# Hybrid encoder layer: one more pair of input columns ahead of the scan, gates clipped inside the scan step, level 8 issued behind level 64, low parts of filler weights apart

## The chip, the cores and the metric

The kernel runs on one core of a Trainium2 chip. The metric is the device time of one execution in microseconds. Before the change it was 1707.46 us, the median of three runs (1707.11 to 1707.71).

## What is computed

One layer on x of 1024 tokens by 1024 channels, in float32:

```
h    = RMSNorm(x);  P = h @ W_in      # 1024 -> 8192 columns
A    = pointwise(silu(LayerNorm(dwconv31(GLU(P_glu)))))
B    = bidirectional gated scan over 8 heads of 128
       S_t = diag(f_t) S_{t-1} + k_t v_t^T,  o_t = S_t^T q_t
       f = clip(lb + (1 - lb) sigmoid(z), 1e-6, 1),  k = (1 - lb) sigmoid(-z)
       then RMSNorm per head * silu(out gate), @ o_w
x    = x + W_out(sigmoid(gA) * A + sigmoid(gB) * B)
x    = x + W_down(silu(dwconv3(h2 W_gate)) * (h2 W_up)),  h2 = RMSNorm(x)
out  = RMSNorm(x)
```

## The kernel before

**Products.** For TensorE (PE) each operand is split into a high part and a low part of type float32r: `split` (L125) casts the high part on ScalarE (ACT) and subtracts it on VectorE (DVE) for the low part. `mm3` issues three matmuls of 512 columns for one product of 128 x 128 weights with 512 tokens: high by high (L149), high by low (L150), low by high (L151). The program counts its PE work in **pieces** of six such matmuls. A column tile of 128 outputs over all 1024 tokens is 8 pieces (48 matmuls) with `std_job` (L251). `pair_job` (L293) does two column tiles together by a Strassen-Winograd scheme of seven products in place of eight: 14 pieces (84 matmuls) in place of 16 (96), with more sums of tiles around them, on DVE, on ACT and, for pairs that are not "first", by accumulating DMAs that GpSimd (POOL) issues (L302).

**Order.** PE's order is the order in which the program issues (`manual_schedule`); the other engines' orders are made by a scheduler, except where `pin` or `issue_after` hold an instruction. A `Stream` is a generator of pieces; `fill(n)` issues n of them, and n may be a fraction that accumulates. So constants such as `FILL` say how much dense work is put between two steps of something else.

**Stages.** The first norm and its transposes (from 0 us; in `warm` and ahead of it PE runs matmuls on a constant that nobody reads, while it waits for x); the GLU tiles (to about 110 us); the depthwise convolution of 31 taps, which DVE does as 120 multiply-adds of 1024 columns (L1065) while PE works through the pairs of the input projection (`conv_steps`, `CONV_FILL` pieces for each tap); the LayerNorm of the convolution with the last pairs (`conv_norm`, to about 475 us); then the scan (from about 498 to 850 us), and after it the output projection, the merge, W_out, the FFN and the last norm.

The 56 column tiles of the input projection that GLU doesn't take are the list `todo`. The first 2 x `NPAIRS` = 38 go through pairs ahead of the scan, and the other 18 (`rest`) are filler within the scan, as `std_job`s, together with the 8 column tiles of the pointwise product.

**The scan.** There are 16 steps, one for each head and each half (512) of the tokens. For both directions at once a chunk is doubled from level to level: at level h, keys kG and queries qF of blocks of h tokens are multiplied by block totals tb (`double_keys`, `double_queries`, `totals`, all recorded at L1194 through `tt`), and ACT copies interleaved pages of them (`woven`, L1228) for PE's small matmuls of the scores (`level`, L1247). Level 1 to 16 are `scan_base`, a generator of five steps; levels 32 and 64 are `scan_levels`, and `scan_states` transposes the level-64 keys (L1382, copied by ACT at L1385), multiplies them with the values (L1392), and makes forward and backward states (L1400, L1410 and then L1491). When both halves of a head are done, `scan_outputs` multiplies the scores and states (L1433, half 1 first), takes squares on ACT (L1438), a power on POOL (L575, L576), scales the result on ACT (L1452), transposes it (L1460) and gates it on DVE (L1462).

Three steps are interleaved by hand. In the step of half i, `between(n)` is called five times; each call issues `FILL` pieces of filler, one step of the outputs of the head before (`pending`), and one step of the base of a following half: the first step (n = 4) of half i + 2, and steps two to five (n = 0 to 3) of half i + 1. `scan_inputs` loads q and the gates' z, and ACT makes kG (L1215), the sigmoid (L1216) and f (L1217); DVE clips f there (L1218). In `Base.step` the first step is held behind the level-64 keys of the half at hand:

```python
            while n > 0 and self.val is None:
                if self.first and last_keys:
                    with tc.issue_after(last_keys[0].ins):
                        self.val = next(self.gen)
```

Halves alternate. While the scores of a half 0 are under way PE does the output matmuls L1433 of the head before, for its half 0, and afterwards their transposes L1460; below, an **A-half** is the stretch from the end of those L1433 to the scores `sc` L1247 of the next half.

Of the kernel before, what the change touches and what calls it, by code (L numbers as in the profile page):

```python
# [10 lines left out]
F32 = mybir.dt.float32  # L11
# [5 lines left out]
AX = mybir.AxisListType  # L17

P = 128
FILL = 1.77  # L20
TAIL = ((1, 2), (1, 1), (2, 4), (2, 3))
CONV_FILL = 1.53
NPAIRS = 19
LN_MEAN = 5
GLU_FIRST = 4
GLU_LEAD = 6
GLU_FILL = 2
GLU_MORE = 4
GLU_LATE = 17
WARM = ((2, 0), (1, 3), (2, 6), (4, 8))  # L30
ALIGN = 128
AHEAD = 55
H = 512
EPS = 1e-6
MIN_FORGET = 1e-6
# [13 lines left out]
def tile_hybrid_encoder(  # L49
# [74 lines left out]
    def split(hi, lo, src, eng, late=False):  # L124
        parts = A.copy(hi, src), eng.tensor_tensor(lo, src, hi.bitcast(F32), op=ALU.subtract)  # L125
        if late:
            for i in parts:
                pin(i)
        return hi, lo
# [9 lines left out]
    def w_page(nk, pool=None):  # L139
        if pool is None:  # L140
            return mp.tile([P, nk, P], F32R, tag="wp", name=nm("wp"), bufs=4)
        return pool.tile([P, nk, P], F32R, tag="wq", name=nm("wq"), bufs=3)
# [105 lines left out]
            while not self.done:  # L248
                self.fill()

    def std_job(src, nk, acts, evac, halves=(0, 1), step=2):  # L251


        def prep():
            raw = raw_w(src, nk)
            return split(w_page(nk), w_page(nk), raw, V)

        def run(w, halves=halves):
            for half in halves:
                acc = bank("mm")  # L260
                for k in range(nk):
                    mm3(acc, w, acts(k, half), k, k == 0, k == nk - 1)
                    if k % step == step - 1 or k == nk - 1:
                        yield
                evac(half, acc)

        return prep, run
# [297 lines left out]
    def in_cols(c0):  # L565
        return w_cols(w_in, 0, ND, c0)
# [570 lines left out]


    rest = todo[2 * NPAIRS :]
    rest_jobs = [std_job(in_cols(c), ND, h_std, e) for c, e in rest[:-2]]  # L1140
    (c0, e0), (c1, e1) = rest[-2:]
    rest_jobs.append(duo_job(in_cols(c0), in_cols(c1), ND, h_std, e0, e1))
    ca = [[None, None] for _ in range(NCW)]
# [30 lines left out]
        return loads, run  # L1174

    rest_jobs.append(pw_first())
    rest_jobs += [std_job(pw_col(i), NCW, ca_of, gated_a(i)) for i in range(1, ND - 2)]
    rest_jobs.append(
        duo_job(pw_col(ND - 2), pw_col(ND - 1), NCW, ca_of, gated_a(ND - 2), gated_a(ND - 1))
    )  # L1180
# [23 lines left out]
    def scan_inputs(i):  # L1204


        h, half = divmod(i, 2)
        q = page(hp, "q", 2)
        f = hp.tile([P, 2, H], F32, tag="f", name=nm("f"), bufs=2)
        kG = hp.tile([P, 2, H], F32, tag="kG", name=nm("kG"), bufs=3)  # L1210
        nc.sync.dma_start(q, d_q[h][half])
        for d in range(2):
            z = page(hp, "zi", 3)
            nc.sync.dma_start(z, d_z[d][h][half])
            A.activation(kG[:, d, :], z, AF.Sigmoid, scale=-1.0)  # L1215
            A.activation(z, z, AF.Sigmoid)  # L1216
            A.activation(f[:, d, :], z, AF.Identity, scale=oml_of(d, h), bias=lb_of(d, h))  # L1217
        V.tensor_scalar(f, f, MIN_FORGET, 1.0, op0=ALU.max, op1=ALU.min)  # L1218
        return q, f, kG, kscale[:, h : h + NH + 1 : NH]

    def pairs(t, h, other=H):
# [47 lines left out]
    def scan_base(ins):  # L1269
# [7 lines left out]
        k_d, Q1 = page(hp, "A", 8), page(hp, "A", 8)  # L1277
        tt(k_d, kG[:, 0, :], kG[:, 1, :], ALU.add)
        A1 = woven(kG, 1)
        odd = H // 2  # L1280
        tt(
            pairs(Q1, 1, 0),
# [185 lines left out]

    class Base:
        def __init__(self, ins):  # L1470
            self.gen, self.val, self.first = scan_base(ins), None, True

        def step(self, n):
            while n > 0 and self.val is None:
                if self.first and last_keys:
                    with tc.issue_after(last_keys[0].ins):
                        self.val = next(self.gen)
                else:
                    self.val = next(self.gen)
                self.first = False  # L1480
                n -= 1

        def result(self):
# [643 lines left out]
```

## Time and profile before

| what | value |
|---|---|
| median of the runs | 1707.46 us (1707.11 to 1707.71) |
| the profiled execution's own time | 1706.98 us |
| its span, first to last instruction | 1705.0 us |
| granted TensorE clock, mean | 0.999 |
| PE busy | 1688.6 us, 11719 rows of matmuls |
| DVE busy | 1269.3 us |
| ACT busy | 827.3 us |
| POOL busy | 245.9 us |
| DMA, mean over the span | 180 GB/s |

Times in rows of a timeline are the start and the duration of an instruction in microseconds. The duration of a matmul includes its way through the array, so what one costs in a row of them is read from start to start. "[0.59 <-ACT A L1228]" behind a row is the idle time of its engine ahead of it and the instruction that ended it. A line number is that of the kernel before.

### The profile page before, as it was taken

What the parts mean: (1) busy time and instruction counts of PE and PEld (TensorE: products, weight loads), DVE (VectorE), ACT (ScalarE), POOL (GpSimd) and SP (SyncE); (2) the same over time, 40 slices, a digit from 0 to 9 for tenths busy, and PEclk for the clock granted to TensorE, in tenths of its full rate; (3) what the DMA queues carried; (4) which work ended last, traced back from release to release, by engine and by line L of the source; (5) the groups of instructions that cost most, each with busy time, mean ns of one, the idle gap of its engine ahead of it and who ended that gap; (6) DMA issues with size and microseconds to landing.
All of it is one profiled execution on the core that took longest, in us unless ns stands there. A gap on an engine that the chain in (4) does not pass through costs nothing.

```text
span 1705.0 us, 30406 instructions
## 1 busy us (share of the span) xinstructions
PE 1688.6 (99%) x11719; PEld 1408.2 (83%) x11719; DVE 1269.3 (74%) x1938; ACT 827.3 (49%) x1562; POOL 245.9 (14%) x287
## 2 busy tenths in 40 slices
PE   9999999999999999999999999999999999999998
PEld 6788888888888888888888888888888888888787
DVE  5889899887678888888565467676777776657865
ACT  7454343335476777776432345444344434442334
POOL 1312222200001111111100003122222222000110
PEclk9999999999999999999999999999999999999999
DMA  7887887866573444436797455686777776773842
GB/s 240 284 213 186 191 196 172 205 187 206 165 236 100 139 129 134 129 116 221 241 294 243 128 167 176 153 171 143 172 164 178 164 183 149 237 260 102 212 98 99
DMA packets 332871, 306.17 MB, mean 180 GB/s; under 512 B 17454, under 2 KB 244918, under 8 KB 332726
## 3 DMA queue, kind: packets, MB, share of 16 engines
q1 hardware_dynamic: 285366, 265.42, 48.8%
q0 software_dynamic: 47360, 38.81, 15.4%
q8 instruction: 92, 1.51, 0.4%
q14 instruction: 53, 0.43, 0.1%
HBM read 201.40 MB, written 84.93 MB: 168 GB/s over the span
## 4 chain that ended last, share of the span: by engine, by line
PE 70%; ACT 1%; DVE 1%; DMA 0%; issue 0%; POOL 0%; POOLq 0%; ACTq 0%; DVEq 0%
PE mm L149 16%; PE mm L151 16%; PE mm L150 16%; PE sc L149 3%; PE sc L150 3%; PE sc L151 3%; PE ob L1433 2%; PE tr L149 2%; PE tr L150 2%; PE tr L151 2%; PE sc L1247 1%; PE sc L1333 1%; PE mm L1392 1%; PE sc L1392 1%; PE ob L1247 1%; PE tr L1382 0%
## 5 line engine op out<-in xcount | busy, mean ns | idle before, releaser
L149 PE MATMUL mm<-hx,wp 128*128 128x512 f32 x1068 | 425.7, 399 | 0.0
L151 PE MATMUL mm<-hx,wp 128*128 128x512 f32 x1068 | 417.0, 390 | 0.5 <-DVE wp L125 0.5
L150 PE MATMUL mm<-hx,wp 128*128 128x512 f32 x1068 | 416.2, 390 | 0.6 <-POOL hx L125 0.6
L125 ACT CAST wp<-wr 128x1024 fp32r<-128x1024 f32 (+2 forms) x146 | 146.9, 1006 | 224.3 <-PE mm L150 165.0
L151 PEld LDWEIGHTS mm<-hx,wp 128*128 128x128 f32 x1068 | 200.5, 188 | 44.6 <-DVE wp L125 1.6
L149 PEld LDWEIGHTS mm<-hx,wp 128*128 128x128 f32 x1068 | 200.6, 188 | 40.6 <-ACT wp L125 0.2
L150 PEld LDWEIGHTS mm<-hx,wp 128*128 128x128 f32 x1068 | 200.8, 188 | 39.9 <-POOL hx L125 1.0
L125 DVE TENSOR_TENSOR wp<-wr,wp 128x1024 fp32r<-128x1024 f32 (+2 forms) x144 | 169.5, 1177 | 39.8 <-ACT wp L125 39.4
L1065 DVE SCALAR_TENSOR_TENSOR acc<-gl,v_b,acc 128x1024 f32<-128x1024 f32 x120 | 153.5, 1280 | 1.7
L441 ACT COPY su<-mm 128x512 f32<-128x512 f32 x82 | 47.8, 583 | 84.4 <-PE mm L151 84.3
L1371 POOL DMA_DIRECT2D S<-D x64 | 36.1, 571 | 281.1 <-ACT jk L1438 125.3
L125 ACT CAST wq<-sw 128x1024 fp32r<-128x1024 f32 x41 | 43.2, 1054 | 61.3 <-PE mm L150 32.9
L1194 DVE TENSOR_TENSOR qF<-qF,tb 128x512 f32<-128x512 f32 x96 | 65.9, 686 | 9.5 <-ACT A L1228 8.9
L149 PE MATMUL tr<-hx,wp 128*128 128x512 f32 x180 | 70.1, 390 | 0.0
L151 PE MATMUL tr<-hx,wp 128*128 128x512 f32 x180 | 70.1, 389 | 0.0
L150 PE MATMUL tr<-hx,wp 128*128 128x512 f32 x180 | 70.0, 389 | 0.0
L1194 DVE TENSOR_TENSOR kG<-kG,tb 128x512 f32<-128x512 f32 x96 | 65.9, 687 | 4.0 <-ACT A L1228 2.2
L1710 DVE SCALAR_TENSOR_TENSOR tm<-gp,v_a,tm 128x512 f32<-128x512 f32 x88 | 66.0, 750 | 3.3 <-ACT tm L1708 1.3
L302 POOL DMA_DIRECT2D sw<-in_ffn_w_up_dram x38 | 49.8, 1502 | 116.0 <-DMA sw<-in_ffn_w_up_dram 72.4
L149 PE MATMUL sc<-hy,wq 128*128 128x512 f32 x164 | 63.9, 390 | 0.0
L151 PE MATMUL mm<-hy,wp 128*128 128x512 f32 x164 | 63.8, 389 | 0.0
L149 PE MATMUL mm<-hy,wp 128*128 128x512 f32 x164 | 63.8, 389 | 0.0
(377 smaller groups left out, 3721.9 us busy)
## 6 DMA issues: line engine op xcount, KB each, us to landing
wr<-in_w_in_dram SPq DMA_DIRECT2D x48, 512.0 KB, 5.6
wr<-in_ffn_w_up_dram SPq DMA_DIRECT2D x22, 512.0 KB, 5.6
sw<-in_w_in_dram SPq DMA_DIRECT2D x38, 256.0 KB, 3.1
d_g<-ft SPq DMA_DIRECT2D x38, 256.0 KB, 2.0
sw<-in_ffn_w_up_dram SPq DMA_DIRECT2D x38, 256.0 KB, 3.2
sw<-in_ffn_w_up_dram POOLq DMA_DIRECT2D x38, 256.0 KB, 6.7
wr<-sw POOLq DMA_DIRECT2D x32, 256.0 KB, 3.2
wr<-wr POOLq DMA_DIRECT2D x32, 256.0 KB, 3.3
```

Of the source, the lines that this page charges most:

```text
L125: parts = A.copy(hi, src), eng.tensor_tensor(lo, src, hi.bitcast(F32), op=ALU.subtract)
L149: T.matmul(acc, whi[:, k, :], ahi, start=first, stop=False, skip_group_check=again)
L150: T.matmul(acc, whi[:, k, :], alo, start=False, stop=False, skip_group_check=again)
L151: T.matmul(acc, wlo[:, k, :], ahi, start=False, stop=last, skip_group_check=again)
L302: G.dma_start(o, a, accum_op=ALU.add)
L441: A.copy(t, acc)
L1065: V.scalar_tensor_tensor(acc, g[:, k : k + S], tap(k), acc, op0=ALU.mult, op1=ALU.add)
L1194: return V.tensor_tensor(o, a, b, op=op)
L1247: T.matmul(b[g, o], A_t[:, at : at + 32], Q_t(at), start=True, stop=True)
L1371: G.dma_start(S_t[g : g + 32, :, g : g + 32], D_t[g : g + 32])
L1392: T.matmul(u[:, sl], kTs[d][:, sl], v[:, c, :], start=True, stop=True)
L1710: V.scalar_tensor_tensor(c, g[:, o + k : o + k + H], vec("fdw", k * NF + j), c, op0=ALU.mult, op1=ALU.add,)
```

## The change

- `NPAIRS` 19 to 20: two column tiles leave the filler and become a twentieth pair, ahead of the scan; `CONV_FILL` 1.53 to 1.64 spreads the pairs over the taps.
- `FILL` 1.77 to 1.57: less filler between the steps of the scan.
- `std_job` gets `apart`: for the filler jobs but the first (and the duo), the cast to the high part is issued two pieces after the load, and the subtraction for the low part a piece later, where both were issued with the load.
- The clip of f moves from `scan_inputs` into `scan_base`, behind the copy of the level-1 keys.
- `Base.step` holds the fourth step (masks of the near levels, the doubling of level 8, the pages of level 16) behind the level-64 keys of the half at hand as well.
- At the start 104 instead of 55 small matmuls run ahead of x, and none instead of two wide ones behind them.

```diff
-FILL = 1.77
+FILL = 1.57
-CONV_FILL = 1.53
-NPAIRS = 19
+CONV_FILL = 1.64
+NPAIRS = 20
-WARM = ((2, 0), (1, 3), (2, 6), (4, 8))
+WARM = ((0, 0), (1, 3), (2, 6), (4, 8))
-AHEAD = 55
+AHEAD = 104
...
-    def std_job(src, nk, acts, evac, halves=(0, 1), step=2):
+    def std_job(src, nk, acts, evac, halves=(0, 1), step=2, apart=False):
         def prep():
             raw = raw_w(src, nk)
-            return split(w_page(nk), w_page(nk), raw, V)
+            if not apart:
+                return split(w_page(nk), w_page(nk), raw, V)
+            hi, lo = w_page(nk), w_page(nk)
+            def low():
+                V.tensor_tensor(lo, raw, hi.bitcast(F32), op=ALU.subtract)
+            def high():
+                A.copy(hi, raw)
+                later(1, low)
+            later(2, high)
+            return hi, lo
...
-    rest_jobs = [std_job(in_cols(c), ND, h_std, e) for c, e in rest[:-2]]
+    rest_jobs = [std_job(in_cols(c), ND, h_std, e, apart=n > 0) for n, (c, e) in enumerate(rest[:-2])]
...
-    rest_jobs += [std_job(pw_col(i), NCW, ca_of, gated_a(i)) for i in range(1, ND - 2)]
+    rest_jobs += [std_job(pw_col(i), NCW, ca_of, gated_a(i), apart=True) for i in range(1, ND - 2)]
...
-        V.tensor_scalar(f, f, MIN_FORGET, 1.0, op0=ALU.max, op1=ALU.min)
         return q, f, kG, kscale[:, h : h + NH + 1 : NH]
...
         A1 = woven(kG, 1)
+        V.tensor_scalar(f, f, MIN_FORGET, 1.0, op0=ALU.max, op1=ALU.min)
...
-            self.gen, self.val, self.first = scan_base(ins), None, True
+            self.gen, self.val, self.at = scan_base(ins), None, 0
...
-                if self.first and last_keys:
+                if self.at in (0, 3) and last_keys:
                     with tc.issue_after(last_keys[0].ins):
                         self.val = next(self.gen)
                 else:
                     self.val = next(self.gen)
-                self.first = False
+                self.at += 1
```

In the changed kernel the lines from `std_job` on stand 12 further down, those between the clip's old and new place 11, and those behind it 12 again. DVE's order in an A-half late in the scan, before: f is the forget gate of the half after next, kG_7922 and qF_8241 the keys and queries of the half at hand (shapes x8x32 level 32, x4x64 level 64), kG_8263 and qF_8620 those of the next half (x128x2 level 2, x64x4 level 4, x32x8 level 8), wp the low part of a filler weight, ev the gated output, D the scores.

```order
L1218 TENSOR_SCALAR f_8636<-f_8636 128x1024
L1194 TENSOR_TENSOR kG_7922<-kG_7922,tb_8584 128x2x8x32
L1194 TENSOR_TENSOR qF_8241<-qF_8241,tb_8584 128x2x8x32
L1194 TENSOR_TENSOR kG_8263<-kG_8263,tb_8633 128x2x128x2
L1194 TENSOR_TENSOR qF_8620<-qF_8620,tb_8633 128x2x128x2
L1194 TENSOR_TENSOR kG_8263<-kG_8263,tb_8735 128x2x64x4
L1194 TENSOR_TENSOR qF_8620<-qF_8620,tb_8735 128x2x64x4
L1462 SCALAR_TENSOR_TENSOR ev_8775<-tr_8770,v_a,og_8541 128x512
L125 TENSOR_TENSOR wp_8754<-wr_8751,wp_8753 128x1024
L1194 TENSOR_TENSOR kG_8263<-kG_8263,tb_8845 128x2x32x8
L1311 COPY_PREDICATED D_8621<-m_d,sc_8778 128x128
L1194 TENSOR_TENSOR kG_7922<-kG_7922,tb_8711 128x2x4x64
```

The same place on DVE now; the half at hand is kG_8033 and qF_8341, the next one kG_8364 and qF_8720:

```order
L1206 TENSOR_TENSOR kG_8033<-kG_8033,tb_8688 128x2x8x32
L1206 TENSOR_TENSOR qF_8341<-qF_8341,tb_8688 128x2x8x32
L1206 TENSOR_TENSOR kG_8364<-kG_8364,tb_8734 128x2x128x2
L1206 TENSOR_TENSOR qF_8720<-qF_8720,tb_8734 128x2x128x2
L1206 TENSOR_TENSOR kG_8364<-kG_8364,tb_8829 128x2x64x4
L1206 TENSOR_TENSOR qF_8720<-qF_8720,tb_8829 128x2x64x4
L1474 SCALAR_TENSOR_TENSOR ev_8863<-tr_8858,v_a,og_8635 128x512
L1206 TENSOR_TENSOR kG_8033<-kG_8033,tb_8811 128x2x4x64
L1206 TENSOR_TENSOR qF_8341<-qF_8341,tb_8811 128x2x4x64
L1323 COPY_PREDICATED D_8721<-m_d,sc_8866 128x128
L1206 TENSOR_TENSOR kG_8364<-kG_8364,tb_8933 128x2x32x8
```

The clip is gone from the head of the row, and the level-64 keys stand ahead of the level-8 keys, a masked copy and the low part of a filler weight, which all stood ahead of them.

PE's order at the end of the first A-half, before: mm is filler, and the transposes of the outputs (tr, from tm) stand right ahead of the scores.

```order
L150 MATMUL mm_5876<-hx_691,wp_5529 128x512
L151 MATMUL mm_5876<-hx_690,wp_5530 128x512
L149 MATMUL mm_5876<-hx_710,wp_5529 128x512
L150 MATMUL mm_5876<-hx_711,wp_5529 128x512
L151 MATMUL mm_5876<-hx_710,wp_5530 128x512
L149 MATMUL mm_5876<-hx_730,wp_5529 128x512
L150 MATMUL mm_5876<-hx_731,wp_5529 128x512
L151 MATMUL mm_5876<-hx_730,wp_5530 128x512
L149 MATMUL mm_5876<-hx_750,wp_5529 128x512
L150 MATMUL mm_5876<-hx_751,wp_5529 128x512
L151 MATMUL mm_5876<-hx_750,wp_5530 128x512
L1460 MATMUL tr_5918<-ident,tm_5685 128x128 x4
```

The same place on PE now, with the transposes of the values (tr from tm_5955) at the head:

```order
L1556 MATMUL tr_6049<-ident,tm_5955 128x128 x4
L149 MATMUL mm_6020<-hx_988,wp_5479 128x512
L150 MATMUL mm_6020<-hx_989,wp_5479 128x512
L151 MATMUL mm_6020<-hx_988,wp_5480 128x512
L149 MATMUL mm_6020<-hx_1060,wp_5479 128x512
L150 MATMUL mm_6020<-hx_1061,wp_5479 128x512
L151 MATMUL mm_6020<-hx_1060,wp_5480 128x512
L1472 MATMUL tr_6062<-ident,tm_5843 128x128 x4
```

Between the transposes of the values and those of the outputs stands one piece of filler here, where two stood. Over the whole A-half, from the end of L1433 to the scores, the order has seven pieces in each of the six A-halves before, and now six, six, seven, six, six, seven. PE's 512-column matmuls number 84 more ahead of the scan and 96 fewer within it.

ACT's order in an A-half, from the copy of the outputs to the level-4 pages (tm L1435 and its squares L1438, kT L1385, a page L1228, an input L1215, L1216, L1217 here and there, the scales L1452, then the pages of levels 2 and 4), has the same instructions before and now, but for the cast of a filler weight that stood in some of them.

## Prediction

> **What bounds the kernel now.** First the page: the shares of the engines.
>
> ```profile
> span 1705.0 us, 30406 instructions
> PE 1688.6 (99%) x11719; PEld 1408.2 (83%) x11719; DVE 1269.3 (74%) x1938; ACT 827.3 (49%) x1562; POOL 245.9 (14%) x287
> ```
>
> PE is busy for 1688.6 of 1705.0 us, so the time is PE's work plus the few waits that it has. Work is priced from start to start: two rows of the timeline with six 512-column matmuls from the one to the other.
>
> ```profile
> 429.62 0.39 PE L150 MATMUL mm<-hy,wq 128*128 128x512 f32 x1
> 430.98 0.39 PE L150 MATMUL mm<-hy,wq 128*128 128x512 f32 x1
> ```
>
> (430.98 - 429.62) / 6 = 0.2267 us for a matmul, so 1.36 us for a piece of six. The Trainium skill, in "TensorE: Matmul & The Clock Gate", section "Wait — 56ns, not 53.3ns?", gives 215.7 ns for 512 columns on the full clock; this trace has 226.7, and the measurement decides.
>
> Next the waits of PE, longest sums first; the columns are total, times, longest.
>
> ```profile
> PE mm L502 <- DMA vr<-in_attn_norm_w_dram: 2.3, 1, 2.3
> PE tr L1382 <- DVE kG L1194: 1.4, 2, 1.1
> ...
> PE sc L1247 <- ACT A L1228: 0.6, 1, 0.6
> ```
>
> Two lines are of the scan: the level-64 keys from DVE (1.4) and the interleaved pages from ACT (0.6), 2.0 us together. The first is the start and isn't touched. So the scan is tight, but PE hardly ever waits in it. The chain of waits says by what it is tight: in an A-half it leaves PE.
>
> ```profile
> 558.84 2.47 PE ob L1433 x22
> 561.33 0.60 ACT tm L1435
> ...
> 565.42 1.67 POOL ors L576
> ...
> 567.88 0.88 ACT tm L1452 x3
> ...
> 575.25 0.53 ACT A L1228
> 575.80 0.59 DVE qF L1194
> ...
> 580.40 0.55 PE tr L1382 x3
> ```
>
> From the end of the output matmuls at 561.33 the work goes through ACT, POOL's power, ACT's scales, the gates' inputs and pages, to the level-4 page at 575.78: 14.45 us, in which PE has only its filler to do. From there DVE carries it to the level-64 keys and PE waits at 580.40.
>
> **The change part by part.**
>
> *Work.* The pair adds 84 matmuls ahead of the scan and the scan loses 96: 12 x 0.2267 = 2.72 us less. Nothing hides that, PE being the bound: -2.72.
>
> *The pair ahead of the scan.* It needs sums and casts on DVE, beside the taps.
>
> ```profile
> 83.00:370.00 287.00, 287.00 (x1268) 237.73 (x1267) 251.23 (x250) 111.62 (x153) 56.89 (x52) 1.00 0.80 192
> ```
>
> The taps' group on the page:
>
> ```profile
> L1065 DVE SCALAR_TENSOR_TENSOR acc<-gl,v_b,acc 128x1024 f32<-128x1024 f32 x120 | 153.5, 1280 | 1.7
> ```
>
> In the stretch of the taps PE is busy without a gap (287.00 of 287.00) and DVE for 251.23, 88%. A pair takes 84 x 0.2267 = 19.0 us, and 287 / 19.0 = 15.1 pairs share the stretch. Taps aside DVE does (251.23 - 153.5) / 15.1 = 6.5 us for one. With a pair more it has some 258 us in 306, 84%: less dense than before. I price it at 0, hidden by PE's own 19 us; bounds: a gain is excluded, since PE has no gap there to lose, and if its cover is gone once, a tap (1.28) is what stands ahead of a part, so +1.3.
>
> *The start.* More small matmuls, no wide ones.
>
> ```profile
> 2.49 1.65 PE L681 MATMUL mm<-ident 128*32 128x32 bf16 x55
> 4.07 1.03 PE L678 MATMUL mm<-ident 128*128 128x512 bf16 x2
> 4.90 0.43 PE L667 MATMUL sc<-ident,xt 128*128 128x128 f32 x1
> 6.76 0.42 PE L667 MATMUL tr<-ident,xt 128*128 128x128 f32 x1
> 6.97 0.37 PE L667 MATMUL ob<-ident,xt 128*128 128x128 f32 x1
> ...
> 8.50 0.27 PE L667 MATMUL sc<-ident,xt 128*128 128x128 f32 x1
> 8.61 0.27 PE L667 MATMUL tr<-ident,xt 128*128 128x128 f32 x1
> ...
> 10.61 0.49 PE L664 MATMUL mm<-diag,ones_r 128*128 128x128 f32 x2 [0.74 <-DVE rs L652]
> ```
>
> A small one costs (4.07 - 2.49) / 55 = 0.0287, so 104 end at 2.49 + 2.99 = 5.48 and the first transpose of x starts 0.58 later than 4.90. That is hidden by the 0.74 at 10.61, a wait for sums of squares that come from ACT and DVE and not from these transposes: 0. Without that cover it is +0.58.
>
> *Old waits of the scan.* Two things made them. At 580.40 PE waited for the level-64 keys; now these stand ahead of the level-8 keys and of the filler's low part, and the clip no longer stands ahead of everything. At 747.36 the clip had held up DVE:
>
> ```profile
> 743.15 0.70 DVE L1218 TENSOR_SCALAR f<-f 128x1024 f32<-128x1024 f32 x1 [2.21 <-ACT f L1217]
> 747.36 0.46 PE L1247 MATMUL sc<-A,A 128*32 128x32 f32 x32 [0.59 <-ACT A L1228]
> ```
>
> DVE stood 2.21 us behind ACT's f, for a clip that only a later half needs; the keys of levels 2 and 4 queued behind it, ACT's pages behind those, PE behind the pages. The clip's new place is behind the keys' scaling, where f has long been written. I take the whole 2.0 off: -2.0; bounds -2.0 and 0. Behind the level-64 keys the fourth step now waits, with masks and level 8; its pages are asked for only in the next half, so it is priced at 0 here and counts in DVE's share below.
>
> *Casts apart.* Cast and subtraction are the same instructions later. A weight tile is loaded a job ahead, 8 or 16 pieces, and the low part is issued after three: five pieces, 5 x 1.36 = 6.8 us at least, are left as cover. 0.
>
> *What is late next.* PE takes the A-half in less time, and the chain through ACT is as long as it was. Four A-halves, each with PE's scores and ACT's last page that these need (a page of qF, in the last third of the 96 small matmuls):
>
> ```profile
> 575.32 0.46 PE L1247 MATMUL sc<-q,A 128*32 128x32 f32 x32
> 575.59 1.07 PE L1247 MATMUL sc<-A,A 128*32 128x32 f32 x96
> ...
> 618.35 1.04 PE L1247 MATMUL sc<-A,A 128*32 128x32 f32 x94
> ...
> 661.18 1.07 PE L1247 MATMUL sc<-A,A 128*32 128x32 f32 x96
> ...
> 703.76 0.46 PE L1247 MATMUL sc<-q,A 128*32 128x32 f32 x32
> 704.03 0.96 PE L1247 MATMUL sc<-A,A 128*32 128x32 f32 x84
> ```
>
> ```profile
> 575.14 0.63 ACT L1228 COPY A<-qF 128x512 f32<-128x512 f32 x1
> 618.20 0.62 ACT L1228 COPY A<-qF 128x512 f32<-128x512 f32 x1
> 660.40 0.62 ACT L1228 COPY A<-qF 128x512 f32<-128x512 f32 x1
> 702.84 0.62 ACT L1228 COPY A<-qF 128x512 f32<-128x512 f32 x1
> ```
>
> The last third starts some 0.59 behind the first row (64 of 96 in 1.07 less a tail of 0.2). So the page was early by 575.59 + 0.59 - 575.77 = 0.41, then 618.94 - 618.82 = 0.12, 661.77 - 661.02 = 0.75, 704.62 - 703.46 = 1.16 us. One piece less, 1.36, in the first, second, fourth and fifth of six A-halves leaves PE waiting 0.95, 1.24 and 0.20 in the first, second and fourth. The third and sixth keep seven pieces: 0. The fifth (747.36) was 0.59 late and loses 1.36, 1.95 together, but the 2.21 behind f go: 0. Sum +2.4. Bounds: 0, if the cast that stood in some of these chains goes and the scheduler's order gains as much; 2.4 + 1.95 = 4.4, if the clip's idle time only changes its place.
>
> *DVE's share.* Here is the sum row of the stretches from 520 to 850 us.
>
> ```profile
> sum 330.00, PE 328.02 PEld 282.06 DVE 277.81 ACT 236.15 POOL 47.43; mean PE 109.34 PEld 94.02 DVE 92.61 ACT 78.72 POOL 15.81
> ```
>
> A period of two halves (one head) is (703.76 - 575.32) / 3 = 42.8 us, and DVE works 277.81 / 330 x 42.8 = 36.0 of it. Two pieces fewer in each of eight periods leave 42.8 - 2.7 = 40.1 for the same 36.0: 90%. No row shows PE's waits at that density. Below 0 is excluded, since no PE wait is left for it to save; the upper end is the second rival. The nearest row is the stretch of the taps, with 88% and no gap on PE, which speaks for little: I take 0.15 a head, +1.2.
>
> Sum against the profiled execution: 1706.98 - 2.72 - 2.0 + 2.4 + 1.2 = 1705.86. The median of the runs was 1707.46, 0.48 above that execution, so the forecast is 1706.3 us, 0.07% less than before.
>
> **The rivals.**
>
> *All waits vanish.* ACT's chain is shorter by 1.24 us or more in each A-half and DVE's density costs nothing: 1707.46 - 2.72 - 2.0 = 1702.7, faster. For it: POOL's power alone is 1.67 of the chain, so half of that gap filled with casts or inputs would do. Against: ACT's instructions in the chain are the same. It counts as faster by over 0.2% (3.4 us, about what a measurement of this kernel can tell from no change) with new waits under 1.3 us.
>
> *DVE becomes the scan's clock, and the time is longer.* DVE idled 42.8 - 36.0 = 6.8 us a period, in waits of which these are the largest between 520 and 850 us:
>
> ```profile
> DVE f L1218 <- ACT f L1217: 10.0, 6, 3.6
> DVE qF L1194 <- ACT A L1228: 8.4, 9, 2.2
> DVE D L1362 <- PE ob L1247: 6.3, 4, 2.2
> ```
>
> Those for the clip go: 10.0 over 330 / 42.8 = 7.7 periods, 1.3 each. If all the others are round trips that stay, a period is 36.0 + 6.8 - 1.3 = 41.5, 1.4 above PE's 40.1, and eight cost 11.2: 1702.7 + 11.2 = 1713.9. It decides from 1.0 a period (new waits of 8.1 us) on. For it: level 8 now queues behind level 64 in every half. Against: most of these waits stand while PE has work, so DVE is early there and not late.
>
> *The reorder doesn't do what it says.* The chain's way to 580.40 led over ACT's pages too (575.25), not over DVE's queue alone; if the level-64 keys come no earlier, the old 2.0 stay: 1708.3.
>
> *The clock.* The granted clock doubles between 6.97 and 8.50 here: transposes 0.21 apart (6.76 to 6.97), then 0.11 (8.50 to 8.61). If it came later, some ten transposes and spreads would cost 0.1 more each, with 0.74 of cover partly spent on the 0.58: 1.0 + 0.58 - 0.74 = +0.8, so 1707.1. The Trainium skill, same page, Part 1 on the clock gate, says that the gate counts busy time in a free-running window of 3.4 us and not matmuls; by that rule the change moves nothing, and the trace, with PE busy from 2.49 on, agrees with that.
>
> **How the numbers follow.** The forecast has 0.48, all waits vanish 0.22, DVE as the clock 0.14, no reorder 0.12, the clock 0.04. Same is 0.48 + 0.12 + 0.04 = 0.64, faster 0.22, slower 0.14. The range goes from the first rival, less 0.6 for its own scatter (the runs before lie 0.6 apart: 1702.1), up to new waits of 8.8, a little past the point where the second one decides (1702.7 + 8.8 = 1711.5); most of that rival and a bit of the first lie outside, under 2 in 10.
>
> **What would show it.** Right: PE's matmuls of 512 columns are 12 fewer; the wait of L1382 for kG is gone; the row of PE's scores waiting for ACT's pages has grown from 0.6 to about 2.4 in three or four A-halves; the period is 40.1 plus some tenths. Wrong: a PE wait ahead of 475 us that names a low part or a sum; the period at 41 or more with DVE named; or no wait in the scan at all.

## The result and the profile after

The changed kernel takes 1713.66 us (median of six runs, 1711.26 to 1716.25) against 1707.37 before (six runs, 1706.88 to 1707.92): a ratio of 1.0038, 95% interval 1.0029 to 1.0048. It is slower by 6.3 us, and its runs lie 5.0 us apart where those of before lie 1.0 apart. The forecast was 1706.3. In what follows one execution, of the kernel with the new amounts of work alone, is left out: it took 6036.71 us at a granted clock of 0.27, and no other is like it.

The profiled execution took 1714.14 us, with a span 7.3 us longer than before. The page's first lines:

```profile
span 1712.3 us, 30481 instructions
PE 1689.3 (99%) x11754; PEld 1408.0 (82%) x11754; DVE 1267.3 (74%) x1946; ACT 830.6 (49%) x1564; POOL 250.9 (15%) x287
```

DVE does as much as before, and POOL 5.0 us more with the same 287 instructions. What PE waits for between 500 and 880 us (total, times, longest):

```profile
PE sc L1258 <- ACT A L1239: 6.3, 8, 1.3
PE mm L151 <- DVE wp L261: 0.8, 1, 0.8
PE ob L1445 <- DVE Sb L1503: 0.5, 1, 0.5
PE mm L151 <- DVE wp L125: 0.3, 1, 0.3
```

The wait for the level-64 keys (L1382, now L1394; 1.4 us before) is gone, as the reorder meant. The wait for ACT's pages has grown from 0.6 to 6.3 us, all in A-halves. Next the chain that ended last, in the first A-half, the one that the prediction showed at 558.84 to 580.40:

```profile
574.20 2.47 PE ob L1445 x22
576.70 0.59 ACT tm L1447
...
580.49 0.54 POOL ors L587
...
581.11 2.25 POOL ors L588
...
583.39 1.28 ACT tm L1464 x4
...
591.56 0.53 ACT A L1239
```

From ACT's copy of the outputs at 576.70 to the level-4 page of the queries at 592.09 are 15.4 us, where 14.45 were. POOL's power (L576, now L588) takes 2.25 where it took 1.67, and its first instruction (L587) 0.54 where it took 0.25. PE's own rows there, on the timeline:

```profile
589.32 0.46 PE L1258 MATMUL sc<-q,A 128*32 128x32 f32 x32
...
590.35 0.46 PE L1258 MATMUL sc<-A,A 128*32 128x32 f32 x32 [0.26 <-ACT A L1239]
592.13 0.46 PE L1258 MATMUL sc<-A,A 128*32 128x32 f32 x32 [1.33 <-ACT A L1239]
...
594.39 0.63 PE L149 MATMUL mm<-hx,wp 128*128 128x512 f32 x1
594.82 0.63 PE L150 MATMUL mm<-hx,wp 128*128 128x512 f32 x1
...
597.12 0.40 PE L150 MATMUL mm<-hx,wp 128*128 128x512 f32 x1
597.36 0.39 PE L151 MATMUL mm<-hx,wp 128*128 128x512 f32 x1
```

After the two waits the 512-column matmuls stand 0.43 us apart (594.39 to 594.82) and not 0.24 as a little later (597.12 to 597.36). That is the granted clock; in the view of stretches the third number from the right is the granted clock:

```profile
590.00:592.00 2.00, 0.54 (x42) 0.35 (x32) 1.72 (x3) 1.84 (x5) 0.00 (x0) 1.00 0.55 181
592.00:594.00 2.00, 1.87 (x51) 1.55 (x52) 1.89 (x4) 1.71 (x5) 0.00 (x0) 0.85 0.17 59
594.00:596.00 2.00, 2.00 (x6) 1.61 (x5) 2.00 (x6) 0.68 (x2) 1.54 (x3) 0.50 0.50 176
596.00:598.00 2.00, 2.00 (x10) 1.58 (x10) 0.60 (x3) 2.00 (x4) 0.70 (x2) 0.80 0.41 141
```

PE worked 0.54 of the 2 us from 590 on, and from about 593.4 to 596.8 it had half a clock: what the three rows lack to 1.00 is 0.15 x 2 + 0.50 x 2 + 0.20 x 2 = 1.7 us lost. Before, no stretch of the scan is under 1.00.

Where the 7.3 us are can be read at places that both orders have: the scan's scores and the transposes of its keys. Their rows, before and then now, give the first and the last start.

```profile
L1247 PE MATMUL sc<-q,A x512: 196/196/218, 497.6 to 811.0; 128*32 128x32 f32 x171
L1382 PE MATMUL tr<-ident,kG x56: 272/273/332, 519.2 to 836.3; 128*128 128x128 f32 x56
```

```profile
L1258 PE MATMUL sc<-q,A x512: 196/196/218, 517.2 to 819.8; 128*32 128x32 f32 x171
L1394 PE MATMUL tr<-ident,kG x56: 270/273/273, 537.4 to 842.3; 128*128 128x128 f32 x56
```

The scan begins 19.6 us later (517.2 against 497.6), of which the pair's own work is 19.0: 0.5 lost ahead of it. From the first scores to the last transposes are 836.3 - 497.6 = 338.7 us before and 842.3 - 517.2 = 325.1 now, 13.6 less, where PE's order has 16 pieces (21.8 us) less: 8.2 lost. Behind it 868.7 became 870.0: 1.3 lost. The work itself is 19.0 - 21.8 = -2.7, and -2.7 + 0.5 + 8.2 + 1.3 = 7.3. So nearly all of the loss lies within the scan.

### The profile page after: what moved, and what is told of

Read it like the earlier page. It is cut to its first block, busy times and chain, and to the rows that moved or that the text cites. A ratio compares the mean times of both kernels' runs of the same rounds, so it can differ in the third digit from the quotient of the medians.

```text
span 1712.3 us, 30481 instructions
## 1 busy us (share of the span) xinstructions
PE 1689.3 (99%) x11754; PEld 1408.0 (82%) x11754; DVE 1267.3 (74%) x1946; ACT 830.6 (49%) x1564; POOL 250.9 (15%) x287
## 4 chain that ended last, share of the span: by engine, by line
PE 63%; ACT 5%; DVE 2%; POOL 1%; issue 1%; DMA 0%; POOLq 0%; ACTq 0%; DVEq 0%
PE mm L149 15%; PE mm L151 15%; PE mm L150 14%; PE sc L149 3%; PE sc L151 3%; PE sc L150 3%; PE ob L1445 2%; PE tr L149 1%; PE tr L151 1%; PE tr L150 1%; ACT A L1239 1%; PE sc L1258 1%; ACT tm L1464 1%; POOL ors L588 1%; PE sc L1345 1%
## 5 line engine op out<-in xcount | busy, mean ns | idle before, releaser
L149 PE MATMUL mm<-hx,wp 128*128 128x512 f32 x1044 | 416.8, 399 | 0.2 <-DVE ev L840 0.2
L151 PE MATMUL mm<-hx,wp 128*128 128x512 f32 x1044 | 408.4, 391 | 1.7 <-DVE wp L125 0.9
L150 PE MATMUL mm<-hx,wp 128*128 128x512 f32 x1044 | 407.7, 391 | 0.6 <-POOL hx L125 0.6
L125 ACT CAST wp<-wr 128x1024 fp32r<-128x1024 f32 (+2 forms) x128 | 130.1, 1017 | 218.3 <-PE mm L150 168.7
L151 PEld LDWEIGHTS mm<-hx,wp 128*128 128x128 f32 x1044 | 196.4, 188 | 45.5 <-DVE wp L125 2.1
L149 PEld LDWEIGHTS mm<-hx,wp 128*128 128x128 f32 x1044 | 196.5, 188 | 40.4 <-DVE ev L840 0.6
L150 PEld LDWEIGHTS mm<-hx,wp 128*128 128x128 f32 x1044 | 196.6, 188 | 38.9 <-POOL hx L125 1.0
L125 DVE TENSOR_TENSOR wp<-wr,wp 128x1024 fp32r<-128x1024 f32 (+2 forms) x126 | 150.2, 1192 | 28.8 <-ACT wp L125 22.8
L149 PE MATMUL tr<-hx,wp 128*128 128x512 f32 x184 | 71.7, 390 | 0.0
L151 PE MATMUL tr<-hx,wp 128*128 128x512 f32 x184 | 71.6, 389 | 0.0
L150 PE MATMUL tr<-hx,wp 128*128 128x512 f32 x184 | 71.6, 389 | 0.0
L1239 ACT COPY A<-kG 128x512 f32<-128x512 f32 x80 | 51.3, 641 | 31.5 <-DVE kG L1206 30.7
L151 PE MATMUL mm<-hy,wp 128*128 128x512 f32 x168 | 65.4, 389 | 0.0
```

Source lines behind the costliest of these rows:

```text
L149: T.matmul(acc, whi[:, k, :], ahi, start=first, stop=False, skip_group_check=again)
L150: T.matmul(acc, whi[:, k, :], alo, start=False, stop=False, skip_group_check=again)
L151: T.matmul(acc, wlo[:, k, :], ahi, start=False, stop=last, skip_group_check=again)
L1239: A.copy(pairs(t_h, h, 0), pairs(t, h))
```

## The experiments

Three theories were tried. **A:** the chain of an A-half (outputs, ACT's squares, POOL's power, ACT's scales, inputs and pages, and from these DVE's level-64 keys) is longer than the filler that PE has there. **B**, the prediction's second rival: DVE has become the pace of the scan. **C:** the edits of the order themselves cost, by late low parts or by level 8 behind level 64. Each ratio is to runs of the kernel before on the same chip, with its 95% interval. **Scan loss** is a sum that I made for each run: the scan's order is cut at the scores and the key transposes into 47 stretches; from each stretch's time 1.36 us are taken off for each of its pieces, and then the shortest rest that any run had for that stretch; what is left is added up. It is 3.7 us for the kernel before and 11.9 for the changed one. It comes from one profiled execution of each kernel.

**Order alone.** The changed kernel with the old amounts of work.

```diff
-FILL = 1.57
+FILL = 1.77
-CONV_FILL = 1.64
-NPAIRS = 20
+CONV_FILL = 1.53
+NPAIRS = 19
```

> The changed kernel with the amounts of work put back: 19 pairs, 1.77 pieces of filler a step and 1.53 pieces a tap, so PE's matmuls and the seven pieces of every A-half are those of before, and only the order of the scan, the casts apart and the start differ. Theory A (the chain from the output matmuls through ACT and POOL to the pages of the scores is longer than the filler of an A-half, and costs waits there): with seven pieces a period is 42.8 us again, PE's waits for pages are 0 to 2 us in sum, the wait for the level-64 keys is gone, and the time is 1705.0 to 1707.5. Theory B (DVE is the pace of the scan): DVE's 36 us fit into 42.8 as they did, 1705.4. Theory C (the order of the edits themselves costs, by level 8 behind level 64 or by late low parts): 1710 or more.

1708.93 us, 1.0009 (1.0000 to 1.0018), scan loss 4.4. The wait for keys fell from 1.4 to 0.6, the wait for pages rose from 0.6 to 1.5:

```profile
PE sc L1258 <- ACT A L1239: 1.5, 3, 0.8
PE tr L1394 <- DVE kG L1206: 0.6, 2, 0.4
```

The edits only move the wait from DVE's end of the chain to ACT's. The time is 1.4 us above what theory A gave it, and no gain. With the old amounts of work POOL's two instructions already take 2.2 to 2.8 us here, and the chain to the level-4 pages 15.1 on the mean of six A-halves, where the kernel before has 2.0 and 14.3.

**Work alone.** The kernel before with the new amounts.

```diff
-FILL = 1.77
+FILL = 1.57
-CONV_FILL = 1.53
-NPAIRS = 19
+CONV_FILL = 1.64
+NPAIRS = 20
```

> The kernel before with the amounts of work alone changed: 20 pairs, 1.57 and 1.64, and the old order, casts, clip and start. Theory A: A-halves of six pieces meet a chain of 14.4 us, and the clip still blocks DVE: waits of 1.36 less what was spare in four halves, 2.4, and the old 2.0 with 1.4 more behind the clip: 1707.4 - 2.7 + 2.4 + 1.4 = 1708.5, up to 1712 if the chain gets longer as in the changed kernel. Theory B: DVE has the clip's waits on top, a period of 41.5 to 42.8, 1714 to 1724. Theory C: without the edits all is well, 1704.7.

1711.53 us (median of seven), 1.0027 (1.0017 to 1.0038), scan loss 10.0, the wait in another place:

```profile
PE tr L1382 <- DVE kG L1194: 4.7, 3, 1.7
PE sc L1247 <- ACT A L1228: 0.7, 2, 0.4
```

So the six pieces cost nearly as much with the old order; C is not needed for most of the loss. Nor is a longer power: POOL's two instructions take 1.9 to 2.1 us in five of the six A-halves, as before, and the chain to the pages is 13.9 on the mean. The loss sits at the other end, where DVE has the level-64 keys late. In the A-half of the longest such wait the chain begins with ACT's copy at 617.97, and PE waits 1.73 us ahead of the last of these rows:

```profile
621.72 0.20 POOL ors L575
...
622.00 1.73 POOL ors L576
...
635.93 0.55 PE tr L1382 x3
```

**Seven, and eight, pieces in each A-half.** The changed kernel with the same filler, laid out by place (for eight: 2.0 and 1.283).

```diff
-                dense.fill(FILL)
+                dense.fill(1.75 if (n >= 3) == (half == 0) and n != 2 else 1.45)
```

> The changed kernel with the same filler, but laid out by place: 1.75 pieces in each of the four steps of an A-half, so seven in each, and 1.45 in the six others. Theory A: four A-halves get 1.36 us more, so of 6.4 us of waits for pages some 1.5 to 3 are left, and the half-clock stretch that followed such a wait goes: 1707 to 1709.5. Theory B: the period is DVE's, where filler stands makes no difference: 1713 to 1714. Theory C: 1713 to 1714 too.

> As the one before it with 2.0 pieces in each step of an A-half, eight in each, and 1.283 in the others. Theory A: the chain of some 15.4 us finds 16.2 us of PE's work: no waits for pages, 1704 to 1707, if the other halves, with seven or eight pieces where they had nine to ten, do not start to wait for DVE (the backward states and the scores); such waits would be named. Theory B: 1713 to 1714. Theory C: 1713 to 1714.

With seven 1711.03 us, 1.0023 (1.0013 to 1.0033), scan loss 8.4: waits for pages 2.0. With eight 1714.95, 1.0050 (1.0036 to 1.0064), scan loss 11.4: none for pages, but the other halves, which gave their filler, now wait for the backward states (3.7), and a late low part waits 1.9:

```profile
PE ob L1445 <- DVE Sb L1503: 3.7, 5, 1.2
PE mm L151 <- DVE wp L261: 1.9, 1, 1.9
```

A holds for the A-halves; but the whole head is now short of filler, and moving it only trades places. Seven missed A's 1707 to 1709.5; eight missed 1704 to 1707, by the waits that its expectation had named as the condition.

**No power.** This shortens the chain instead of filling it. The kernel leaves out the root in the norm of the heads, so it computes something else and is no version to use.

```diff
 def rstd_small(dst, ss, n, late=False):
+    if n == DK:
+        V.tensor_scalar(dst, ss, 1.0 / n, EPS, op0=ALU.mult, op1=ALU.add)
+        V.reciprocal(dst, dst)
+        return
```

> The changed kernel with the power of the heads' norm left out of the scan: POOL's two instructions are replaced by a scaling and a reciprocal on DVE, so the outputs are normed by the mean square and not by its root. Theory A (the chain of an A-half is the bound there, and 2.4 to 3.4 us of its 15.3 are POOL's two instructions, longer than the 1.95 of before): the chain becomes some 12.5 to 13 us, under the 13.5 of six pieces; of 6.4 us of waits for pages at most 0.5 is left, no half-clock stretch, and the time is 1704 to 1707. Theory B (DVE is the pace): DVE gets more work, 1713 to 1715. Theory C (late low parts and level 8): 1713.

1704.75 us, 0.9983 (0.9974 to 0.9991), scan loss 4.0: 8.9 us less than the changed kernel, and no wait that names ACT's pages is left among its waits from 500 to 870 us ("issue" marks a wait for which the profile shows no releaser):

```profile
PE mm L151 <- DVE wp L261: 0.9, 1, 0.9
PE mm L151 <- issue: 0.9, 1, 0.9
PE ob L1449 <- DVE Sb L1507: 0.5, 1, 0.5
PE sc L1262 <- issue: 0.3, 1, 0.3
```

DVE has more to do in it than in the changed kernel (1270.2 us against 1267.3). So B falls here: DVE's own work is not the pace of the scan.

**The three edits of the order, each taken back.** Three kernels: casts and low parts with the load; level 8 free; the clip back in the inputs.

```diff
-    rest_jobs = [std_job(in_cols(c), ND, h_std, e, apart=n > 0) for n, (c, e) in enumerate(rest[:-2])]
+    rest_jobs = [std_job(in_cols(c), ND, h_std, e, apart=False) for n, (c, e) in enumerate(rest[:-2])]
...
-    rest_jobs += [std_job(pw_col(i), NCW, ca_of, gated_a(i), apart=True) for i in range(1, ND - 2)]
+    rest_jobs += [std_job(pw_col(i), NCW, ca_of, gated_a(i)) for i in range(1, ND - 2)]
...
-                if self.at in (0, 3) and last_keys:
+                if self.at == 0 and last_keys:
...
+        V.tensor_scalar(f, f, MIN_FORGET, 1.0, op0=ALU.max, op1=ALU.min)
         return q, f, kG, kscale[:, h : h + NH + 1 : NH]
...
         A1 = woven(kG, 1)
-        V.tensor_scalar(f, f, MIN_FORGET, 1.0, op0=ALU.max, op1=ALU.min)
```

> The changed kernel with the casts and low parts of the filler issued with the load again. Theory A: the chain gets a cast (1 us) back in some A-halves, the late low parts (0.84 and 0.34 us of waits behind 810 us) go: 1712 to 1714. Theory B: 1713 to 1714. Theory C: 1709 to 1711.

> The changed kernel without the wait of level 8 for the level-64 keys. Theory A: DVE takes level 8 earlier and the level-64 keys later; waits for keys of 1 to 3 us come back, waits for pages stay 4 to 6: 1713 to 1716. Theory C: 1708 to 1711, since the edit itself is the cost.

> The changed kernel with the clip back where it was, right behind ACT's f. Theory A with POOL held up by a busy DVE: DVE is idle again ahead of the clip while POOL takes the power, so POOL's two instructions fall from 2.4 to 3.4 us to about 2, the chain is 13.5 to 14.5 and the waits for pages are 1 to 3; but what queues behind the clip is late, and the waits for the level-64 keys return with 2 to 5: 1710 to 1713. If POOL's time does not depend on DVE: POOL stays at 2.8 and the waits for pages at 6, 1714 to 1717.

1713.29 us, 1.0032 (1.0019 to 1.0044); 1714.36, 1.0040 (1.0027 to 1.0053); 1713.83, 1.0040 (1.0026 to 1.0053): none differs from the changed kernel by more than the runs scatter. With the casts or the clip taken back the waits for pages stay (6.6 in both). With level 8 free the wait only shifts: the keys are late again, and less is waited for the pages:

```profile
PE tr L1394 <- DVE kG L1206: 5.3, 4, 1.9
PE sc L1258 <- ACT A L1239: 2.1, 3, 0.8
```

In that kernel POOL's two instructions take 2.1 to 2.4 us in five of six A-halves and 3.5 in the third, and nothing is gained by it. With the clip back POOL's two instructions still took 2.7 to 3.2 us and the waits for pages 6.6, so the clip is not what kept POOL's time short before; that part of the expectation missed. So C falls for each edit by itself; all of them together cost the 1.6 us of the order alone.

**The power by itself.** A kernel that does nothing of the layer: POOL's two instructions, with DVE idle or working without a gap.

```diff
+    for busy, n in ((None, 0), (tt, 40), (ts, 40), (stt, 20), (psum, 32)):
...
+        for _ in range(8):
+            G.tensor_scalar(rs, rs, 1.0 / DK, EPS, op0=ALU.mult, op1=ALU.add)
+            G.tensor_tensor(rs, rs, mhalf.to_broadcast([P, 2, 4]), op=ALU.pow)
```

> None of the layer is computed: POOL does the two instructions of the heads' norm (scale and add, power, on 128 x 8) eight times in each of five stretches, and DVE does nothing, or products of 128 x 512 within SBUF, or clips of 128 x 1024, or multiply-adds of 128 x 1024, or gated products of 128 x 512 that read PSUM, one right behind the other. Theory A with POOL held up by a busy DVE: 0.2 + 1.66 us with DVE idle, and 0.5 to 1.5 more where DVE works without a gap, with some kinds of instruction if not with all. If POOL's time does not depend on DVE: 1.86 in each stretch.

POOL's rows with DVE idle, with products within SBUF, with multiply-adds within SBUF (1285 ns each), and with products that read PSUM:

```profile
7.41 0.20 POOL L123 TENSOR_SCALAR rs<-rs 128x8 f32<-128x8 f32 x1
7.68 1.63 POOL L124 TENSOR_TENSOR rs<-rs,mhalf 128x8 f32<-128x8 f32 x1
...
25.71 0.66 POOL L123 TENSOR_SCALAR rs<-rs 128x8 f32<-128x8 f32 x1
26.45 2.08 POOL L124 TENSOR_TENSOR rs<-rs,mhalf 128x8 f32<-128x8 f32 x1
...
87.21 1.12 POOL L123 TENSOR_SCALAR rs<-rs 128x8 f32<-128x8 f32 x1
88.41 2.67 POOL L124 TENSOR_TENSOR rs<-rs,mhalf 128x8 f32<-128x8 f32 x1
...
113.48 0.20 POOL L123 TENSOR_SCALAR rs<-rs 128x8 f32<-128x8 f32 x1
113.76 1.63 POOL L124 TENSOR_TENSOR rs<-rs,mhalf 128x8 f32<-128x8 f32 x1
```

1.83 us become 2.74 and 3.79 with DVE busy in SBUF (2.74 with clips too), and stay 1.83 where DVE reads one operand from PSUM. So each of POOL's instructions is longer by something under one DVE instruction.

**The wait filled.** Twelve transposes of a constant ahead of the scores of each A-half.

```diff
         b = bank("sc")
+        seen.append(1)
+        if len(seen) > 4 and len(seen) % 2 == 1:
+            for _ in range(12):
+                T.transpose(b[:, :P], ident, ident)
```

> The changed kernel with twelve transposes of a constant (1.3 us of PE, into a bank that the scores then overwrite) ahead of the scores in each A-half. PE waits 1.3 us less for pages in each and has 1.3 us more to do. Theory A with the clock: the six A-halves that wait as long or longer lose nothing by it, the shorter waits lose the rest (about 2 us in sum), and the half-clock stretch of 3.4 us (1.6 us lost) does not come: 1713 to 1715, with the runs closer together than 1711 to 1716. If the clock is untouched by such waits: 1715 to 1717.

1715.84 us (1714.28 to 1716.64), 1.0050 (1.0037 to 1.0063). Waits for pages fell from 6.3 to 1.3, and the granted clock is 0.998 or 0.999 in its five runs, where it is 0.996 to 0.998 in the six of the changed kernel. So such waits can cost clock, and that is a likely part of the changed kernel's scatter. They need not: the kernel with the clip back waits as long at the same place (0.26 and 1.33 us), PE works 0.49 of the same 2 us, and its profiled execution keeps the whole clock there:

```profile
590.00:592.00 2.00, 0.49 (x36) 0.38 (x37) 1.60 (x4) 1.84 (x5) 0.00 (x0) 1.00 0.58 140
```

The median of the kernel with filled waits lies where the expectation put it for an untouched clock, though the clocks say otherwise: what the clock gave back was less than the transposes cost in the halves with short waits. As a test of the size of the clock's cost it is inconclusive.

**The power of half 1 early.** Each half of a head gets its own power, half 1's right behind its squares, and its scales come first.

```diff
+            rstd_small(rs[:, half], ss[:, half], DK)
             if half == 1:
                 yield
-        rstd_small(rs, ss, DK)
...
-        for half in range(2):
+        for half in (1, 0):
             for c in range(4):
```

> The changed kernel with the norm of each half of a head by itself: the power of half 1 is taken right behind its squares, 20 us earlier, and its four scales come ahead of those of half 0. The chain of an A-half loses four scales (1.2 us) on ACT and keeps POOL's two instructions. Theory A: waits for pages fall from 6.4 by 1.2 in each of the halves that wait longer, to 1 to 3: 1707 to 1710. Theory B: 1713 to 1714.

> The early power of half 1, seven pieces of filler in each A-half by place, and the pointwise filler's low parts with their load again. Theory A: the chain of some 14.1 us finds 14.9 us of PE's work, waits for pages at most 0.5, the waits for late low parts behind 810 us gone, waits for backward states 1 to 1.5 left: 1703.5 to 1706.5, below both kernels. Theory B: 1713.

Alone on the changed kernel: 1708.63 us, 1.0010 (1.0000 to 1.0019), scan loss 6.5. With seven pieces and the pointwise filler not apart: 1709.36, 1.0010 (1.0001 to 1.0019), scan loss 5.8, against 1703.5 to 1706.5 expected. The first took 5.0 us off without touching DVE's work or PE's. No wait that names the pages is left in it, though waits of 1.4 us at the scores have no releaser in the profile, and its scan loss of 6.5 is still above the 3.7 of the kernel before. In the second the waits for pages are gone too, but 1.5 us for backward states, 1.4 for kT's copies and some starts are left, and its runs are not better than the first's. The cause of that difference I did not find.

**The early power at 19 pairs**, and with the low parts together.

> The kernel before with nothing changed but the norm of the heads' halves: half 1's power right behind its squares, and its scales ahead of half 0's. Theory A (the chain of an A-half is what the scan's waits hang on, at 19 pairs too): the chain loses four scales, 1.2 us; the waits for the level-64 keys and the pages (2.0 us in sum before) go to at most 0.7, 1705 to 1706.5. If the waits of before come from the clip and from level 8 ahead of level 64 alone: no change, 1707.4.

> The order edits at 19 pairs (the first experiment) with the early power. Theory A: its waits for pages (1.5) and keys (0.6) go, 1706 to 1707. Otherwise 1708.9 as there.

> The changed kernel with the early power, and the pointwise filler's casts with their load again. The late low parts behind 809 us (0.87 and 0.4 us of waits, more with their starts) go: 1707 to 1707.5, against 1708.6. If they are no cost: 1708.6.

> As the first of these four, with the filler laid out by place: 1.75 in each step of an A-half, seven in each, 1.783 in the others. Theory A: where the chain fits already this gains nothing: 1705 to 1707.

On the kernel before: 1706.14 us, 0.9993 (0.9984 to 1.0001), scan loss 1.5; with seven pieces by place (1.75 and 1.783) 1705.49, 0.9989 (0.9980 to 0.9998), scan loss 1.6. Both lose every wait of the scan; from 500 to 870 us one is left, behind it:

```profile
PE mm L149 <- ACT wp L125: 0.4, 1, 0.4
```

For seven pieces the edit is `FILL` to `1.75 if (n >= 3) == (half == 0) and n != 2 else 1.783`. The order edits at 19 pairs with the early power: 1706.57, 0.9997 (0.9988 to 1.0006), scan loss 1.8, from 1708.93 without. The changed kernel with it and with the pointwise low parts together: 1707.76, 1.0003 (0.9994 to 1.0012), 0.9 less than with them apart, which is within the scatter of both; the wait of 0.87 at 809 us is gone. So the chain was what the kernel before waited for as well. The version with seven pieces and the early power at 19 pairs is faster than the changed kernel, and by 1.6 us, about 0.1% and just clear of its interval, than the kernel before.

## Why the prediction was wrong

*Work:* right, 12 matmuls fewer. *The start:* 0 forecast, and 0 in the end: the first products start 0.18 later (14.58 against 14.40), and a shorter wait at 73.3 us takes that back. The clock doubled earlier than before, not later: transposes are 0.11 apart from 6.37 on. *The pair ahead of the scan:* 0 forecast, 0.5 measured, inside its bound of 1.3; 0.22 of it is a new wait for DVE (ev, L840) at 261.95 us.

*Old waits of the scan:* the keys' 1.4 went, as said. That they went because the clip no longer blocks DVE is not shown: with the clip taken back the keys did not wait either. Level 8 did it: set free, the keys wait 5.3.

*Casts apart:* wrong, if small. I took five pieces of cover; a low part of the pointwise filler came 0.84 late at 814 us and another 0.34 behind the scan. Undoing them for the pointwise filler on top of the early power gave 0.9 less, which the scatter does not let pass for shown.

*What is late next* is the step that failed. The place, the wait (scores for ACT's pages) and the method held; of the halves, three were forecast and five waited. The size did not hold: 2.4 forecast and 6.3 in rows. I took the chain "as long as it was". It is longer in five of six A-halves: from ACT's copy to the level-4 page 14.4, 14.7, 14.1, 13.4, 15.6, 13.8 us before (mean 14.3) and 15.4, 15.1, 15.6, 15.6, 14.6, 15.1 now (15.2).

The mean grew by 0.9, and POOL's two instructions grew by that on the mean: from 2.0, 1.9, 1.9, 2.0, 2.3, 1.9 to 2.9, 2.9, 3.4, 3.4, 2.8, 2.4. What stands ahead of POOL takes 3.8 before and now, and what stands behind it 8.5 on the mean of both; single halves differ there by more (7.6 to 9.4 before, 8.0 to 9.0 now), because casts are gone, the order of ACT's instructions moved, and DVE's keys hold ACT up in some.

Put into the prediction's own margins (0.41, 0.12, 0.75, 1.16, -0.59; the sixth 1.09 by the same reading), these lengths and pieces give waits of 1.9, 1.6, 0.7, 2.4, 1.0 and 0.2, 7.8 us; the stretches of the scan loss, the 1.6 of the slow clock taken off the first, show 1.9, 1.6, 0.8, 2.2, 1.2 and 0.3, 8.0 (the 6.3 of the waits leaves out the restart behind each). So the prediction's upper bound of 4.4 was too low because it let only PE's side move.

ACT has the same instructions but for the cast, though not quite in the same order: in the first A-half the gate f (L1217) ran while POOL took the power, at 564.89, and now (L1229) stands behind the first scales, at 584.57. POOL's durations could not be read from the order, and they depend on what DVE does in those 2 us. Here is DVE beside POOL's two instructions in the first A-half, before (POOL from 565.09 to 567.08), then after (580.49 to 583.35):

```profile
565.23 1.11 DVE L1400 SCALAR_TENSOR_TENSOR Sf<-Sf,Tt,sc 128x128 f32<-128x128 f32 x3
568.50 0.64 DVE L1362 COPY_PREDICATED D<-m,ob 128x128 f32<-128x128 uint8 x2 [2.15 <-PE ob L1247]
```

```profile
580.28 0.68 DVE L1206 TENSOR_TENSOR kG<-kG,f 128x512 f32<-128x512 f32 x1
...
581.14 0.68 DVE L1206 TENSOR_TENSOR qF<-A,f 128x512 f32<-128x512 f32 x1
...
582.00 0.68 DVE L1206 TENSOR_TENSOR tb<-f 128x512 f32<-128x512 f32 x1
```

Before, DVE reads PSUM and then stands idle for 2.15 us; now it works without a gap, at the next half's products within SBUF and, between them, at the state updates that read PSUM. A fuller DVE by itself does not do it: with the work alone POOL takes 1.9 to 2.1 us in five of six A-halves. The new order does part of it: with the order alone, at the old amounts of work, POOL takes 2.4 on the mean, and with both 2.9. That it is level 8's new place in that order fits the kernel with level 8 free.

But the longer power is not needed for a loss of this size: it says why the pages are as late as they are in the changed kernel. With the work alone the pages cost 0.7 and the keys 4.7, at a scan loss of 10.0; with level 8 free the pages cost 2.1 and the keys 5.3. So the chain goes on through DVE to the keys, and the order decides at which end of it PE waits. No run takes away what DVE adds to POOL and nothing else, so its own share of the time stays open.

*The clock* was weighed at the start only. In the profiled execution waits of 0.26 and 1.33 us within the scan were followed by 1.7 us of lost clock; the kernel before had no wait of that length at its scores, and no term held that. Not every such wait does it, as the kernel with the clip back shows.

*DVE's share:* 1.2 forecast, 0.5 in the wait for the backward states, and more with its start. *DVE as the clock:* its time, 1713.9, is close to the measured one and its period of 41.5 to the 41.8 that the first rows show, (714.69 - 589.32) / 3. But its mechanism is not what happened, so its time fits by luck: with more on DVE and POOL out of the chain the time is 1704.75. DVE matters by what it does when, by holding up POOL in one order and by making the keys late in the other, and not by the sum of its work. *All waits vanish* names the right condition for the pages, a shorter chain: with the early power at 20 pairs no wait that names them is left. Its time of 1702.7 did not come: other waits remain there, and the kernel takes 1708.63.

The scores of the fourth A-half, three periods behind those at 589.32, wait twice as well:

```profile
714.69 0.46 PE L1258 MATMUL sc<-q,A 128*32 128x32 f32 x32
...
716.23 0.46 PE L1258 MATMUL sc<-A,A 128*32 128x32 f32 x32 [0.78 <-ACT A L1239]
717.75 0.46 PE L1258 MATMUL sc<-A,A 128*32 128x32 f32 x32 [1.06 <-ACT A L1239]
```

What stays open: why POOL is held up in some halves for 0.4 us and in others for 1.4, which would need DVE's and POOL's starts to the last 0.1 us; and why seven pieces did not help on top of the early power at 20 pairs but did, by 0.6 us within the scatter, at 19.

## What to carry to other kernels

Where filler is taken out of a loop that is saturated by one engine, list the serial chains that this filler covers, with their length and their spare time, to each end at which the saturated engine waits, and let both sides move: a neighbour with a new order and less time for its work can make the chain itself longer. Shorten such a chain (part of its input is there long before) before removing its cover; here that was worth 5.0 us on the changed kernel, and reordering what stands behind the chain was worth nothing (by itself it made the kernel before 1.6 us slower).

## What the runs showed of the hardware

POOL's small instructions take longer beside some of DVE's: 0.20 + 1.63 us alone, 0.66 + 2.08 beside products of 128 x 512 within SBUF, 1.12 + 2.67 beside multiply-adds of 1.28 us, and nothing beside products that read PSUM. The Trainium skill, "SBUF — State Buffer", section "Who interferes with whom", has the rule: a DVE instruction with two SBUF inputs contends with a GpSimd instruction that reads SBUF, one in a two-port mode contends with GpSimd as well, and one with at most one SBUF input outside these modes does not. The four stretches agree with it.

The granted clock fell to 0.50 for 3.4 us behind waits of 0.26 and 1.33 us with small matmuls between them. The Trainium skill, "TensorE: Matmul & The Clock Gate", section "HAM oscillation — how this bites in real kernels", speaks of idle gaps over some 3.4 us; here a stretch of 2 us with PE busy for 0.54 of it came just ahead of the drop, so the clock dropped sooner than that rule says. It did not drop each time: behind the same waits the kernel with the clip back kept 1.00. That the waits are the cause is supported by the kernel with filled waits, whose clocks stayed up, and not shown beyond that.
